# Four waits in the mixing stages and the order of the last down projection, in a two-layer hybrid backbone with expert-choice routing

## The chip, the cores and the metric

The kernel runs on one core of one Trainium2 chip. A time is device microseconds from the start to the end of one execution. The time before is the median of three runs; beside it there is one profiled execution, from which every row below comes.

## The reference

Two layers work on 512 latent tokens and 256 context tokens of width 1024, all in float32. Each layer mixes tokens and then routes them to 16 experts:

```python
for l in range(DEPTH):
    # six modulation vectors of each stream, from the conditioning
    mod = silu_c @ w_ada[l] + b_ada[l]
    mod_c = silu_cc @ w_ada[l] + b_ada[l]
    ...
    mix_c, st_f, st_b = token_mixer(xn_c @ w_in[l], ...)       # mLSTM, conv, Fourier
    h_ctx = h_ctx + cgt1 * (mix_c @ w_out[l])
    h_ctx = h_ctx + cgt2 * expert_choice_ffn(modulated_rmsnorm(h_ctx, ...), ...)
    mix_x, _, _ = token_mixer(xn @ w_in[l], ...)               # starts from st_f, st_b
    x = x + gt1 * (mix_x @ w_out[l])
    x = x + gt2 * expert_choice_ffn(modulated_rmsnorm(x, ...), ...)
return _rms(x, g_final)

def expert_choice_ffn(xn, w_router, w_gate, w_up, w_down):
    aff = softmax(xn @ w_router)
    gate, idx = top_k(aff.T, 2 * n // 16)      # 64 latent, 32 context tokens an expert
    hid = silu(xs @ w_gate) * (xs @ w_up)      # xs: the rows of xn at idx
    ys = (hid @ w_down) * gate
    return zeros_like(xn).at[idx].add(ys)
```

The last layer mixes the context only as far as its mLSTM states, and routes latent tokens alone.

## The kernel before

Each layer has four stages: the mixing with its input projection, the output projection with the residual, the routing (logits, softmax, the top tokens of each expert, the gather of their rows), and the experts in eight pairs.

**Who sets the order.** TensorE's instructions run in the order in which the code is written. The other engines' instructions are put in order by a scheduler that looks at dependencies and estimated costs, so a line can go much earlier or later than it stands. Each engine then runs its own list strictly in order: an instruction that waits holds up all behind it. Transfers are issued from SP's queue (weights in the main) and from POOL's queue (`w_ada`, the gate rows, gathers).

**Weights of the projections.** Each block of 128 columns of `w_in` or `w_out` is loaded by SP (L414), split into a high half on ScalarE (L422) and a low half on VectorE or, for some blocks, on POOL (L425), and multiplied by TensorE (L490). In layer 1 POOL makes the low half of every second block from number 4 to 15, in layer 0 from 12 to 19.

**The gates of the mLSTM.** A generator computes running sums and maxima of the gates with VectorE scans (L654, L656), then four exponentials on ScalarE (L680 to L690), and writes two results, M and WI, to a scratch tensor in DRAM from POOL's queue (L706, L707). They are fetched back later (L773). The key blocks are copied out of PSUM with a scale by ScalarE at L973.

**Fill work.** The modulation vectors are made from `w_ada` by small matmuls (L284, eight a yield in layer 0's out-projection; one result is copied at L290 and multiplied at L293). This work is a generator that runs between the blocks of other stages. An object of class `Fill` holds a credit: each block adds its time by a rate, and the generator runs while the credit is above zero. The vectors of layer 1 are made from layer 0's output projection on (`ada1`), and what is left of them runs in the routing.

**The output projection** goes over eight blocks `db`. Its residual line is L1177 on VectorE. L1108 scales the router's weights, which L1104 loads, for use on TensorE. Before the loop a tile Z of zeros is written on POOL (L1097) and sent to the accumulators `accl` and `accc` in DRAM (L1099, 3 MB in all); its place is then free for the next tile, which is that of the router's weights. The experts' outputs are added to these accumulators.

**The routing** ends with casts of the chosen indices on ScalarE (L1281, L1285), two small matmuls (L1288), index arithmetic on VectorE, gathers of the rows on POOL's queue (L1356), and TensorE's transposes of them (L1382).

**The experts.** Gate and up are L1433. A pair's two experts sit in the two halves of TensorE's columns (64 tokens each in layer 1), and gate and up take turns between them. `down_last` is the down projection of layer 1's last pair: four quarters `qd` of 256 output columns, 16 matmuls each (L1693). ScalarE scales a quarter out of PSUM (L1699), VectorE makes its low half (L1700). The sums into the residual are made by a permutation matmul for each block of 128 channels (L1498, two matmuls each) and L1499 on VectorE; `scat` is a list of such closures and `pop(scat, n)` runs n of them. ScalarE squares the result (L1675), and `rows` sums the squares on TensorE (L1683) for the final norm. L1693's loop over `k0` and `e` sets four matmuls of one expert, one popped closure, four of the other, another closure.

Of the kernel before, what the change touches and what calls it, by code (L numbers as in the profile page):

```python
# [50 lines left out]
NACC = 6  # L51
WORDER = [[KB0 + i for i in range(4)] + p + [QB + i for i in range(4)] + [FB, FB + 1] + [OB + i for i in range(4)]
# [103 lines left out]
def build(nc, tc, xT, ctxT, params, w_ada, w_gates, w_in, w_out, w_router, w_e_gate, w_e_up, w_e_down,  # L156
# [6 lines left out]
    def body(A, RB, PS, scr, xrow, acc):  # L163
# [233 lines left out]
        for l in range(2):  # L397
# [216 lines left out]
            keep = {}  # L614
            convq = []
# [18 lines left out]
            def chain():  # L634
# [45 lines left out]
                act.activation(DEC, DEC, AF.Exp)  # L680
# [4 lines left out]
                act.activation(WS, WS, AF.Exp)  # L685
                dve.tensor_tensor(FL, b_, M, OP.add)
                act.activation(FL, FL, AF.Exp, scale=-1.0)
                WI = b_
                dve.tensor_tensor(WI.rearrange("p (c t) -> p c t", c=6), MSb, M3, OP.subtract)
                act.activation(WI, WI, AF.Exp)  # L690
# [15 lines left out]
                pool.dma_start(scr[l, 0], M)  # L706
                pool.dma_start(scr[l, 1], WI)  # L707
# [258 lines left out]
            for h in range(H):  # L966
                ps = in_block(KB0 + h, seqs)
                for s in seqs:
                    o, v = tview(kT[:, h, OFF[s]:OFF[s] + LEN[s]], h, s), rview(ps[s], h, s)
                    if h < 2 and s == LAT:  # L970
                        dve.tensor_scalar(o, v, 128.0 ** -0.5, None, op0=OP.mult)
                    else:
                        act.activation(o, v, AF.Copy, scale=128.0 ** -0.5)  # L973
                done.add(f"k{h}")
                if h == 0 and l == 0:
                    areg = [mem.alloc(1024) for _ in range(4)]

                    def ada0():
                        for r in (1, 2):
                            yield from ada_round(0, r, Ring(areg), 5, pool, wloads[1:2] if r == 1 else (), some=ADS[0])  # L980
                        ada_scale(0, A2[0], 4, P_G2)

                    fills.append(Fill(ada0(), ADA0_RATE))
# [111 lines left out]
            if not last:  # L1095
                z_r, Z = new(512)
                pool.memset(Z, 0.0)  # L1097
                for s, a in ((LAT, 8), (CTX, 4)):
                    sp.dma_start(acc[s].rearrange("(p a) (b f) -> p (a b) f", p=128, f=512),  # L1099
                                 Z[:, None, :].to_broadcast([128, a, 512]))  # L1100
                mem.free(z_r)
# [11 lines left out]
            if not last:  # L1113
# [9 lines left out]
                ada1f = Fill(ada1(), ADA1_RATE)  # L1123
                fills.append(ada1f)


# [6 lines left out]
            wtiles, wtaken = [], [0]  # L1133

            def load_experts(firsts=(), most=1000):
                while len(wtiles) < min(wtaken[0] + len(wreg), len(wq), most):
                    w, e, i = wq[len(wtiles)]
                    if last and w is w_e_down and e >= E - 2:
# [3 lines left out]
                        for k0, k1 in ((0, KB),) if i < 3 else ((0, 4), (4, KB)):  # L1142
                            sp.dma_start(t[:, k0:k1], src[:, k0:k1])
# [17 lines left out]
            for db in range(KB):  # L1161
# [14 lines left out]
                for s in outs:  # L1176
                    dve.scalar_tensor_tensor(X[s][:, db], banks[s], MOD[l][:, s, 16 + db:17 + db], X[s][:, db],  # L1177
                                             op0=OP.mult, op1=OP.add)
                if db == 4:
                    ride(0)  # L1180
# [7 lines left out]
            mem.free([YT_r, wraw, wh, wl, wr_r, wra_r])  # L1188
# [473 lines left out]
            def down_last(p):  # L1662
# [23 lines left out]
                for qd in range(4):  # L1686
# [3 lines left out]
                    for k0 in (0, 4):  # L1690
                        for e in range(2):
                            for k in range(k0, k0 + 4):
                                pe.matmul(b[64 * e:64 * e + 64], hT[:, k, 64 * e:64 * e + 64], w[e][:, k],  # L1693
                                          start=k == 0, stop=k == KB - 1, tile_position=(0, 64 * e))
                            pop(scat)
                    pop(scat, 99)
                    c0 = qd * 256
                    h, lo = (YS[:, j, c0:c0 + 256] for j in range(2))
                    act.activation(h, b, AF.Copy, scale=GP[:, 0, p:p + 1])  # L1699
                    dve.scalar_tensor_tensor(lo, b, GP[:, 0, p:p + 1], h.bitcast(F32), op0=OP.mult, op1=OP.subtract)  # L1700
                    if qd == 2:
                        rows(range(4))
                    scat.extend(last_sum(db) for db in (2 * qd, 2 * qd + 1))
# [141 lines left out]
```

## Time and profile before

| | |
|---|---|
| median of three runs | 1856.98 us (1856.57 to 1857.13) |
| the profiled execution's own time | 1857.74 us |
| its span, first to last instruction | 1856.0 us |
| TensorE busy | 1744.3 us, 94% |
| VectorE, ScalarE, POOL busy | 627.9, 448.5, 166.0 us |
| mean granted clock of TensorE | 0.97 of 2.4 GHz |
| moved by DMA | 529.59 MB, mean 285 GB/s |

The span is 1.74 us shorter than the execution's own time: start and end around the instructions. The median is 0.76 us below the profiled execution. Layer 0's mixing lies at about 36 to 450 us, its routing to 482, its experts to 1035; layer 1's mixing runs to about 1340, and its experts to the end. Busy TensorE means that a matmul is in flight, not that the array is full.

### The profile page before, as it was taken

How to read it: one execution, taken by the hardware profiler on the slowest of the kernel's cores; microseconds unless marked ns; L12 is line 12 of the kernel's file. 1: busy time of each engine (PE TensorE's matmuls, PEld its weight loads, DVE VectorE, ACT ScalarE, POOL GpSimd, SP SyncE). 2: the span in 40 equal slices, each digit the busy share in tenths (PEclk: the TensorE clock that was granted, in tenths of full speed). 3: DMA queues.
4: the chain of work that ended last, by engine and by line, in shares of the span. 5: the costliest groups of instructions: out<-in, count | busy, mean ns of one | idle time of the engine just before them, and what ended most of it. 6: DMA issues, size and time to landing. Idle time of an engine off the chain costs nothing.

```text
span 1856.0 us, 27692 instructions
## 1 busy us (share of the span) xinstructions
PE 1744.3 (94%) x11728; PEld 947.8 (51%) x11728; DVE 627.9 (34%) x1384; ACT 448.5 (24%) x862; POOL 166.0 (9%) x193
## 2 busy tenths in 40 slices
PE   7899999899899999999999989889989999999997
PEld 3678887676333333333233468777644444334433
DVE  4624897323201001001014567956230221121213
ACT  5423354313201101101000553346221001110001
POOL 1122120321101101101100001110000000000000
PEclk8999999899899999999999999999989999999998
DMA  9365344855899999999995112233659999999992
GB/s 346 115 208 193 106 133 137 314 188 209 350 419 402 411 412 403 399 421 391 393 393 217 35 54 79 76 108 129 250 240 421 420 420 421 420 421 420 421 420 99
DMA packets 100668, 529.59 MB, mean 285 GB/s; under 512 B 10176, under 2 KB 21440, under 8 KB 51648
## 3 DMA queue, kind: packets, MB, share of 16 engines
q1 hardware_dynamic: 81920, 459.66, 61.8%
q0 software_dynamic: 18624, 68.17, 11.7%
q8 instruction: 92, 1.51, 0.3%
q14 instruction: 32, 0.26, 0.0%
HBM read 513.10 MB, written 14.68 MB: 284 GB/s over the span
## 4 chain that ended last, share of the span: by engine, by line
PE 70%; DMA 10%; DVE 9%; issue 5%; ACT 2%; SPq 2%; POOL 1%; another core or an unknown queue 0%; DVEq 0%; POOLq 0%; ACTq 0%
PE PS L1433 29%; PE PS L490 16%; PE PS L1443 8%; PE PS L1379 3%; DVE A L1015 2%; PE PS L1498 2%; PE PS L284 1%; PE PS L1693 1%; SPq L309 1%; DMA accc<-A 1%; DMA WP<-w_e_up 1%; DMA A<-w_e_up 1%; DMA A<-w_e_down 1%; DMA A<-w_e_gate 1%; DMA WP<-w_e_gate 1%
## 5 line engine op out<-in xcount | busy, mean ns | idle before, releaser
L490 PE MATMUL PS<-RA,RB 128*128 128x512 f32 (+1 forms) x2352 | 516.4, 367 | 23.6 <-ACT A L973 8.0
L1433 PE MATMUL PS<-A 128*32 128x512 f32 (+1 forms) x2256 | 428.1, 594 | 2.7 <-DMA A<-w_e_up 2.2
L490 PEld LDWEIGHTS PS<-RA,RB 128*128 128x128 f32 x2352 | 379.3, 194 | 99.3 <-issue 20.6
L1433 PE MATMUL PS<-WP,A 128*32 128x512 f32 (+1 forms) x2160 | 373.9, 597 | 0.7 <-DMA WP<-w_e_up 0.7
L1433 PEld LDWEIGHTS PS<-A 128*32 128x32 f32 (+1 forms) x2256 | 128.0, 121 | 224.9 <-issue 213.7
L1433 PEld LDWEIGHTS PS<-WP,A 128*32 128x32 f32 (+1 forms) x2160 | 107.0, 117 | 192.7 <-issue 187.6
L1443 PE MATMUL PS<-WP,A 128*32 128x512 f32 x816 | 112.5, 595 | 0.0
L1015 DVE SCALAR_TENSOR_TENSOR A<-A 128x783 f32<-128x783 f32 (+1 forms) x120 | 107.4, 921 | 0.1
L1499 DVE SCALAR_TENSOR_TENSOR A<-PS,A 128x512 f32<-128x512 f32 x80 | 57.5, 748 | 130.5 <-PE PS L1498 130.5
L1387 ACT ACTIVATE A<-PS,A 128x128 f32<-128x128 f32 x80 | 36.4, 457 | 262.0 <-DVE A L1389 260.8
L1486 ACT ACTIVATE A<-PS 128x512 f32<-128x512 f32 x40 | 23.8, 597 | 306.2 <-PE PS L1485 306.0
L1389 DVE TENSOR_SCALAR A<-PS,A 128x128 f32<-128x128 f32 x80 | 32.6, 409 | 185.8 <-PE PS L1382 93.4
L1443 PE MATMUL PS<-A 128*32 128x512 f32 x656 | 95.3, 607 | 0.0
L422 ACT ACTIVATE RB<-A 128x1024 fp32r<-128x1024 f32 x60 | 63.2, 1057 | 128.4 <-PE PS L490 83.1
L1532 DVE TENSOR_SCALAR A<-PS,A 128x512 f32<-128x512 f32 x6 | 4.5, 750 | 245.6 <-PE PS L1433 245.6
L282 POOL DMA_DIRECT2D A<-w_ada x80 | 60.1, 754 | 211.2 <-PE PS L284 134.2
L1506 DVE SCALAR_TENSOR_TENSOR RB<-PS,A,RB 128x512 fp32r<-128x512 f32 x18 | 13.5, 750 | 163.7 <-ACT RB L1505 162.8
L1379 PE MATMUL PS<-A 128*128 128x128 f32 x512 | 64.0, 285 | 5.0 <-DVE A L1499 4.5
L425 DVE TENSOR_TENSOR RB<-A,RB 128x1024 fp32r<-128x1024 f32 x50 | 60.8, 1221 | 21.0 <-ACT RB L422 20.6
L1379 PEld LDWEIGHTS PS<-A 128*128 128x128 f32 x512 | 61.0, 199 | 12.9 <-DVE A L1499 9.8
L1443 PEld LDWEIGHTS PS<-WP,A 128*32 128x32 f32 x816 | 26.8, 109 | 50.8 <-issue 50.8
L1498 PE MATMUL PS<-RB 128*128 128x512 f32 x160 | 51.7, 431 | 1.0 <-DVE A L1499 0.4
(334 smaller groups left out, 1583.8 us busy)
## 6 DMA issues: line engine op xcount, KB each, us to landing
A<-w_e_gate SPq DMA_DIRECT2D x75, 1024.0 KB, 14.3
A<-w_e_up SPq DMA_DIRECT2D x66, 1024.0 KB, 13.0
WP<-w_e_down SPq DMA_DIRECT2D x63, 1024.0 KB, 14.3
A<-w_e_down SPq DMA_DIRECT2D x63, 1024.0 KB, 16.0
WP<-w_e_up SPq DMA_DIRECT2D x62, 1024.0 KB, 13.0
WP<-w_e_gate SPq DMA_DIRECT2D x53, 1024.0 KB, 14.9
A<-w_ada POOLq DMA_DIRECT2D x80, 512.0 KB, 5.5
A<-w_in SPq DMA_DIRECT2D x44, 512.0 KB, 3.7
```

The costliest lines, as they stand in the source:

```text
L282: after(eng.dma_start(w, src[r, hf, k]), firsts if hf == 0 and k < len(ring.regs) else ())
L422: whi.append(act.activation(h, raw[i], AF.Copy))
L425: wlo.append(eng.tensor_tensor(lo, raw[i], h.bitcast(F32), OP.subtract))
L490: pe.matmul(banks[s][:, :LEN[s]], w[:, k], xin[:, j, k, OFF[s]:OFF[s] + LEN[s]], start=k == k0 and i == 0, stop=k == k1 and i == 2)
L1015: dve.scalar_tensor_tensor(o, i, wcol, o, op0=OP.mult, op1=OP.add)
L1379: pe.matmul(b[:, j], XT[2 + c][:, db * 128:db * 128 + 128], onehots[i][:, c], start=c == 0, stop=c == 3)
L1387: act.activation(dst[:, db], b[:, j], AF.Identity, bias=sh_, scale=sc_)
L1389: dve.tensor_scalar(dst[:, db], b[:, j], sc_, sh_, op0=OP.mult, op1=OP.add)
L1433: pe.matmul(B(o + hf)[c:c + wd, :], lhs(k, e)[:, c % 64:c % 64 + wd], w[e][:, a, hf * 512:hf * 512 + 512], start=k == 0, stop=k == KB - 1, ...
L1443: pe.matmul(B(o + 2)[32 * g:32 * g + 32, :], lhsc(k, e), w[e][:, a, hf * 512:hf * 512 + 512], start=k == 0, stop=k == KB - 1, tile_positio ...
L1498: pe.matmul(b, YS[:, j, db * 128:db * 128 + 128], PM if pm is None else pm, start=j == 0, stop=j == 1)
L1499: dve.scalar_tensor_tensor(X[LAT][:, db], b, MOD[l][:, LAT, 40 + db:41 + db], X[LAT][:, db], op0=OP.mult, op1=OP.add)
```

## The change

Five edits:

1. ScalarE's four exponentials of the gates are made to come after a key copy: the generator waits until `k1` is done, and each exponential has a dependency without a semaphore (an order for the scheduler) on the last key copy, which L973 records in `kev`.
2. The two transfers of M and WI are put behind the last splits that POOL has been given.
3. Z takes a place at the top of the memory that is not given to another tile until the end of the output projection. The two transfers of it are written in blocks 1 and 3 of that loop.
4. `ada1f` starts with a debt of 2.0 us of credit.
5. In `down_last` the two experts take turns at each `k`, and closures run after a quarter instead of within it. The loads of the last quarter's weights go half by half for both experts.

```diff
+ADA1_LATE = 2.0
...
+            kev = []
...
-                act.activation(DEC, DEC, AF.Exp)
+
+                while "k1" not in done:
+                    yield None
+                after(act.activation(DEC, DEC, AF.Exp), kev, NOSYNC)
...
-                act.activation(WS, WS, AF.Exp)
+                after(act.activation(WS, WS, AF.Exp), kev, NOSYNC)
...
-                pool.dma_start(scr[l, 0], M)
-                pool.dma_start(scr[l, 1], WI)
+                for j, t in enumerate((M, WI)):
+                    after(pool.dma_start(scr[l, j], t), [w for w in wlo[-2:] if w.ins.engine == mybir.EngineType.Pool], NOSYNC)
...
-                        act.activation(o, v, AF.Copy, scale=128.0 ** -0.5)
+                        kev[:] = [act.activation(o, v, AF.Copy, scale=128.0 ** -0.5)]
...
-            if not last:
-                z_r, Z = new(512)
-                pool.memset(Z, 0.0)
-                for s, a in ((LAT, 8), (CTX, 4)):
-                    sp.dma_start(acc[s].rearrange("(p a) (b f) -> p (a b) f", p=128, f=512),
-                                 Z[:, None, :].to_broadcast([128, a, 512]))
-                mem.free(z_r)
...
+                ada1f.credit = -ADA1_LATE
                 fills.append(ada1f)
 
+            if not last:
+                z_r, Z = new(512, top=True)
+                pool.memset(Z, 0.0)
...
-                        for k0, k1 in ((0, KB),) if i < 3 else ((0, 4), (4, KB)):
-                            sp.dma_start(t[:, k0:k1], src[:, k0:k1])
+
+                        halves.append((t, src))
+                        if i < 3:
+                            sp.dma_start(*halves.pop())
+                        elif len(halves) == 2:
+                            for k0 in (0, 4):
+                                for t_, s_ in halves:
+                                    sp.dma_start(t_[:, k0:k0 + 4], s_[:, k0:k0 + 4])
...
+                if db in (1, 3) and not last:
+
+                    s, a = ((LAT, 8), (CTX, 4))[db // 2]
+                    sp.dma_start(acc[s].rearrange("(p a) (b f) -> p (a b) f", p=128, f=512),
+                                 Z[:, None, :].to_broadcast([128, a, 512]))
...
-                    for k0 in (0, 4):
+
+                    for k in range(KB):
                         for e in range(2):
-                            for k in range(k0, k0 + 4):
-                                pe.matmul(b[64 * e:64 * e + 64], hT[:, k, 64 * e:64 * e + 64], w[e][:, k],
-                                          start=k == 0, stop=k == KB - 1, tile_position=(0, 64 * e))
-                            pop(scat)
-                    pop(scat, 99)
+                            pe.matmul(b[64 * e:64 * e + 64], hT[:, k, 64 * e:64 * e + 64], w[e][:, k],
+                                      start=k == 0, stop=k == KB - 1, tile_position=(0, 64 * e))
...
+                    if qd == 0:
+                        pop(scat, 99)
...
-                    if qd == 2:
+                    if qd == 3:
                         rows(range(4))
+                    pop(scat, 99)
```

In the changed kernel the lines have other numbers: L284 is L285 there, L290 is L291, L293 is L294, L1099 is L1191, L1104 is L1102, L1281 is L1295, L1285 is L1299, L1288 is L1302, L1382 is L1396, L1498 is L1512, L1683 is L1697 and L1693 is L1707.

TensorE's list from the last logits transposes to the gather's transposes in layer 0's routing, first before and then after the change:

```order
L1242 MATMUL PS_70<-A_63,WP4_3275 96x128 x2
L1266 MATMUL PS_70<-A_63 128x128 x48
L284 MATMUL PS_70<-A_63 32x256 x16
L1288 MATMUL PS_70<-A_63,WP5_3276 128x96 x2
L284 MATMUL PS_70<-A_63 32x256 x40
L293 MATMUL PS_70<-A_63 128x8 x4
L1382 MATMUL PS_70<-A_63,WP5_3276 128x128 x8
```

```order
L1256 MATMUL PS_70<-A_63,WP4_3258 96x128 x2
L1280 MATMUL PS_70<-A_63 128x128 x48
L294 MATMUL PS_70<-A_63 128x8 x4
L285 MATMUL PS_70<-A_63 32x256 x8
L1302 MATMUL PS_70<-A_63,WP5_3259 128x96 x2
L285 MATMUL PS_70<-A_63 32x256 x56
L294 MATMUL PS_70<-A_63 128x8 x4
L1396 MATMUL PS_70<-A_63,WP5_3259 128x128 x8
```

One group of L294 has moved from the output projection to the place ahead of L1302, with eight L285 behind it, and 56 instead of 40 stand between L1302 and the transposes. On ScalarE the copy L291 for that first group stands between the two L1295.

TensorE's list in the last down projection, from its first quarter into its second, before and after (WP0 to WP2 and A are the places of the weights):

```order
L1485 MATMUL PS_70<-A_63 128x128 x8
L1693 MATMUL PS_70<-A_63 64x256 x4
L1498 MATMUL PS_70<-RB_64 128x512 x2
L1693 MATMUL PS_70<-WP0_8537,A_63 64x256 x4
L1498 MATMUL PS_70<-RB_64 128x512 x2
L1693 MATMUL PS_70<-A_63 64x256 x4
L1693 MATMUL PS_70<-WP0_8537,A_63 64x256 x4
L1693 MATMUL PS_70<-WP1_8538,A_63 64x256 x4
```

```order
L1707 MATMUL PS_70<-A_63 64x256
L1707 MATMUL PS_70<-WP0_8537,A_63 64x256
L1512 MATMUL PS_70<-RB_64 128x512 x4
L1707 MATMUL PS_70<-WP1_8538,A_63 64x256
L1707 MATMUL PS_70<-WP2_8539,A_63 64x256
L1707 MATMUL PS_70<-WP1_8538,A_63 64x256
L1707 MATMUL PS_70<-WP2_8539,A_63 64x256
```

After the change the first two rows are repeated eight times ahead of the four sums, and so are the pairs of the later quarters; no sum stands within a quarter any more.

SP's list from the start, before and after:

```order
L309 DMA A_63<-w_ada 128x4x256 x8
L414 DMA A_63<-w_in 128x1024 x2
L309 DMA A_63<-w_ada 128x4x256 x8
L414 DMA A_63<-w_in 128x1024 x14
L883 DMA A_63<-dft_ch 128x256
```

```order
L310 DMA A_63<-w_ada 128x4x256 x8
L415 DMA A_63<-w_in 128x1024 x2
L310 DMA A_63<-w_ada 128x4x256 x8
L415 DMA A_63<-w_in 128x1024 x2
L1191 DMA accl_68<-A_63 1024x1x512
L1191 DMA accc_69<-A_63 512x1x512
L415 DMA A_63<-w_in 128x1024 x12
L888 DMA A_63<-dft_ch 128x256
```

The two transfers of zeros now stand behind the fourth load of w_in instead of just ahead of the router's weights. On POOL's list in layer 1 both transfers to `scr` now stand behind two splits, where before the first of them stood ahead of the first split and the second ahead of the second.

## Rows read from the trace of the kernel before

**Rows 1.** The page's part 2: tenths of TensorE's busy time, and GB/s.

```profile
PE   7899999899899999999999989889989999999997
...
GB/s 346 115 208 193 106 133 137 314 188 209 350 419 402 411 412 403 399 421 391 393 393 217 35 54 79 76 108 129 250 240 421 420 420 421 420 421 420 421 420 99
```

**Rows 2.** The chain that ended last, around the last pair: start, us, what.

```profile
1792.34 3.82 PE PS L1433 x16
...
by line: PE PS L1693 45.4%; PE PS L1498 11.9%; DVE A L1747 8.4%; PE PS L1683 4.8%; PE PS L376 3.7%; DVE A L1499 2.7%; PE PS L1433 2.3%; PE PS L359 1.9%; DVE RB L1700 1.8%; ACT RB L1699 1.7%; DVE A L375 1.6%; issue 1.6%; PE PS L1485 1.2%; DV
...
1804.02 1.94 PE PS L1693 x8
1805.96 0.66 PE PS L1498 x2
...
1809.16 2.80 PE PS L1693 x16
...
1812.56 0.49 DVE RB L1700
...
1836.95 0.98 PE PS L1683 x4
...
1838.63 0.76 DVE A L1499
...
1840.15 1.72 PE PS L1683 x4
```

**Rows 3.** L1693's own instructions: weight loads, ns min/median/max.

```profile
L1693 PEld LDWEIGHTS PS<-WP,A x96: 132/137/137, 1806.6 to 1835.4; 128*64 128x64 f32 x96
```

**Rows 4.** The chain that ended last, 325 to 365 us.

```profile
329.04 21.76 DMA accc<-A
...
350.88 7.25 DMA A<-w_router
```

**Rows 5.** Waits, 325 to 365 us: us in total, times, longest.

```profile
PE PS L490 <- DVE A L1177: 4.4, 1, 4.4
...
PE PS L284 <- DMA A<-w_ada: 3.8, 2, 2.9
```

**Rows 6.** Transfers, 0 to 70 us, in 40 slices of 1.75 us.

```profile
GB/s 0 186 305 375 391 362 391 384 387 384 386 384 393 420 393 385 384 389 373 382 404 413 379 370 349 201 5 0 0 0 0 0 0 5 0 227 169 213 187 360
```

**Rows 7.** Timeline of the routing: start, us, instructions, idle before and its releaser.

```profile
466.10 0.63 ACT L1281 ACTIVATE WP<-WP 32x128 f32<-32x128 f32 x2 [1.47 <-DVE WP L1249]
...
467.10 0.39 PE L1288 MATMUL PS<-A,WP 96*128 96x96 f32 x2 [1.63 <-ACT WP L1285]
...
467.41 4.52 PE L284 MATMUL PS<-A 128*32 128x256 f32 x80
...
470.18 1.06 POOL L1356 DMA_INDIRECT WP<-xrow,A  x1 [19.93 <-DVE A L1322]
...
474.63 0.60 ACT L290 ACTIVATE A<-PS 128x512 f32<-128x512 f32 x1 [7.59 <-remote]
...
475.28 1.45 PE L293 MATMUL PS<-A 128*128 128x8 f32 x8 [3.34 <-ACT A L290]
...
476.58 1.95 PE L1382 MATMUL PS<-A,WP 128*128 128x128 f32 x8
```

**Rows 8.** Timeline of the second split in layer 1's mixing.

```profile
1099.65 1.08 ACT L422 ACTIVATE RB<-A 128x1024 fp32r<-128x1024 f32 x1
...
1107.57 2.70 POOL L425 TENSOR_TENSOR RB<-A,RB 128x1024 fp32r<-128x1024 f32 x1
1107.99 2.30 DVE L679 TENSOR_TENSOR A<-A 128x6 f32<-128x6 f32 x1
...
1110.32 7.05 PE L490 MATMUL PS<-RA,RB 128*128 128x512 f32 x22 [5.03 <-POOL RB L425]
...
1114.15 1.23 DVE L425 TENSOR_TENSOR RB<-A,RB 128x1024 fp32r<-128x1024 f32 x1 [2.12 <-ACT RB L422]
```

**Rows 9.** TensorE's waits, 84 to 102 us.

```profile
PE PS L490 <- ACT A L973: 6.8, 1, 6.8
```

More of the change, by code (lines that the diff above doesn't have):

```diff
@@ L684, in chain @@
                                   ML[:, :, None].to_broadcast([128, 6, 128]), OP.subtract)
-                act.activation(WS, WS, AF.Exp)
+                after(act.activation(WS, WS, AF.Exp), kev, NOSYNC)
                 dve.tensor_tensor(FL, b_, M, OP.add)
-                act.activation(FL, FL, AF.Exp, scale=-1.0)
+                after(act.activation(FL, FL, AF.Exp, scale=-1.0), kev, NOSYNC)
                 WI = b_
                 dve.tensor_tensor(WI.rearrange("p (c t) -> p c t", c=6), MSb, M3, OP.subtract)
-                act.activation(WI, WI, AF.Exp)
+                after(act.activation(WI, WI, AF.Exp), kev, NOSYNC)
                 while KGO[l] not in done:
@@ L1132, in body @@
             wq = [(w, 2 * q + e, i) for w, q in order for i in range(4) for e in range(2)]
-            wtiles, wtaken = [], [0]
+            wtiles, wtaken, halves = [], [0], []
             def load_experts(firsts=(), most=1000):
@@ L1187, in body @@
             fills.clear()
-            mem.free([YT_r, wraw, wh, wl, wr_r, wra_r])
+            mem.free([YT_r, wraw, wh, wl, wr_r, wra_r] + ([] if last else [z_r]))
             ra_close()
```

## The prediction

> **What bounds the kernel now.** I read the page's forty slices first [rows 1]. TensorE is at 9 tenths or more in all but nine (46.4 us each): 1, 2 and 8 in layer 0's mixing, 11 with the routing, 24, 26 and 27 in layer 1's mixing, 30 with its routing, and the tail. From slice 31 the transfers stand flat at 420 GB/s, so layer 1's experts are bound by their weights, while in layer 0's experts TensorE never waits. Both stages run as long wherever they begin: time taken out of the mixing before them moves all that follows, and time taken out of the last down projection, after the stream has ended, comes off the end directly. So I price four places, each by the wait that ends last there: layer 0's out-projection, the routing behind it, the splits in layer 1, and the last down. The profiled execution took 1857.74 us, 0.76 above the median of 1856.98; I make the sum on the profile and take 0.76 off.
>
> **The last down, the largest term.** The chain over the last pair [rows 2] shows four quarters of 16 matmuls (64x256; each leaves two records, so x8 is four matmuls). Four matmuls of one expert standing alone, x8, take 1.94, 0.47 each. Eight, four of one expert and then four of the other, take 2.80: the second four add only 0.9. The two experts sit in different column halves, and the halves overlap where both have work queued. Before, the order offers that only partly: a block of one expert, two full-width sums of 0.66, a block of the other, two more sums, then both blocks. L1693 makes 45.4% of these 56 us, 25.4, or 6.35 a quarter, and a quarter's four sums 1.33. The nearest row for full alternation is in the same view: eight 64x512 matmuls of gate or up, alternating, x16, take 3.82. That is as many columns as 16 of 64x256, so I price a quarter at 3.75 and the downs at 15.0 against 25.4, 10.4 less.
>
> Not all of that stays, because the sums lose their cover. My walk from 1804.02, which is unchanged: quarter 0 to 1807.8; four sums (1.33) to 1809.1; quarter 1 shares quarter 0's bank and must wait until VectorE's L1700 has read it. Before, this wait was 1.1 (1811.96 to the 0.49 at 1812.56 and its end); now two updates of 0.76 (L1499) stand in front of that read, so I let it begin at 1810.4. Quarter 1 to 1814.1; sums to 1815.4; quarter 2 to 1819.1; sums to 1820.4; the same wait to 1820.9; quarter 3 to 1824.6. Then four row sums L1683 (0.98), four sums (1.33) to 1826.9, a round trip of L1499, a square (L1675) and row sums that used to lie under matmuls, about 2.4 to 1829.3, the last sums to 1830.6, and the final L1683, after its update, at 1831.5. Before, that one began at 1840.15. **Term: -8.6**, bounds -6.5 (each round trip 1 us longer) and -10.4 (none shows). The last slice, from 1809.6, moves 99 GB/s over 46.4 us, 4.6 MB, of which 2.1 are the result; the other 2.5 are weights, 6 us at 420 GB/s [rows 1]. So the weights are in by 1816, ahead of quarter 3 at 1820.9; if the reordered last halves came after that, each us late would cost one.
>
> Here a rule counts against the change. Each matmul loads its own weights, 64 columns in 132 ns [rows 3]. In the alternating rows 16 loads would add 2.1 to 3.82 if they were exposed, and the row has no room for them, so I count them as hidden. The Trainium skill (TensorE: Matmul & The Clock Gate, part 3, What overlaps and what doesn't) says that a weight load overlaps matmuls in flight only when the row group differs, and these pairs use all rows. By it the gain would be about nil here; the 3.82 of this trace disagrees with it. This is the second rival below.
>
> **Zeros in an own place.** Before, the zeros for the accumulators go out near 329, behind a memset that waits for TensorE; the second transfer lands 21.76 after issue, and the router's weights, whose tile takes the place of the zeros, go only at 350.88 and land 7.25 later [rows 4]. VectorE scales them, L1177 stands behind on its queue, and TensorE waits 4.4 for it [rows 5]. After, the router's load has no such wait and is issued at about 329: on nobody's path. **Term: -4.4**, bounds 0 (something else holds L1177 as long) and -4.4. The zeros, 3 MB, now stand on SP's queue behind four early loads of w_in and ahead of all others. The DMA engines carry next to nothing from about 46 to 60 us, since the tiles of the next w_in are not free yet [rows 6]. So the 3 MB, at the 21.76 they took beside other traffic, fit before the next w_in load at about 60. Cost 0; without that cover, up to 21.8 (the third rival).
>
> **Vectors' fill later.** TensorE waits 3.8 for w_ada in two places [rows 5]: the fill's first loads were issued just before, and the zeros are moving at the same time [rows 4]. The debt of 2.0 at a rate of 0.3 puts the first yield some 7 us later, and the zeros are gone from there. **Term: -3.8**, bounds -2 and -3.8. One group of the fill, 8 of L284 (113 ns each [rows 7]) and four of L293 (at most 1.45 there, I take 1.0), leaves the out-projection, where TensorE is busy: **-1.9**, bounds -1 and -2.3.
>
> They come back in the routing. Before, TensorE's L1288, which passes the chosen indices on, started at 467.10 as soon as ScalarE's casts were done. After, four L294 and eight L285 stand ahead of it on TensorE, and the L294 wait for a copy (0.60) that ScalarE does between the two casts: 466.10 + 0.31 + 0.60, 467.0. So L1302, the same line, starts at 467.0 + 1.2 for L294 + 0.9, near 469.1, 2.0 late, and with it the gather (before: issued from 470.18, used at 476.58 [rows 7]). **Term: +2.1**, lower bound +1.5. The 56 L285 behind it end at 469.6 + 56 x 0.113 = 475.9, the copy and the last L294 near 478.0, inside the gather's new end of 478.7. But before, the copy at 474.63 came 2.7 after the last L284 (467.41 + 4.52) for a reason the trace does not name; if that hold comes again the drain ends at 480.7 and the term is +4.1, the upper bound.
>
> **Rows out behind the splits, in layer 1.** POOL had its queue blocked by L706, which waits for VectorE; behind it stood the split L425, whose input was ready at 1100.7. It ran at 1107.57 for 2.70, and TensorE waited 5.03 for it [rows 8]. After, the splits stand first, so this split can end at 1103.4 and TensorE goes on at 1105.3. But what is late next is the following block's low half, VectorE's L425 at 1114.15 to 1115.4, behind the exponentials; TensorE finishes the earlier block by about 1110.3 and stops there instead. It resumes earlier only if VectorE's chain does. While POOL's split ran, VectorE's L679, of six columns, took 2.30 and ended with it. Move the split to 1100.7 and an operation there is held instead: the scans of the gates. Then VectorE ends as late as before and the gain is 0; if the scans are not held, 2.2. The row with the held operation is nearer, so **-0.4**, bounds 0 and -2.2. The Trainium skill (SBUF — State Buffer, the section on the ports) has the shared port pair as an exclusive lock for a GpSimd operation that reads SBUF and a VectorE operation with two inputs there; scans are of that kind, so by it the term is 0. The 2.30 agrees with it. In layer 0 the rows out keep their place among the same instructions; the first fetch of them moves behind fourteen w_ada issues, still ahead of the second fetch: 0.
>
> **Exponentials behind key copies.** The order shows ScalarE's exponentials between the same key copies in both layers as before. In layer 0 TensorE's 6.8 for the copy L973 [rows 9] is what it was meant for, and the copy still stands behind them: **0**, bounds 0 and -1.
>
> **Sum**: -8.6 - 4.4 - 3.8 - 1.9 + 2.1 - 0.4 = -17.0. On the profile 1840.7, as a median **1840.0**. All best ends together give about -23, all worst ones -5.
>
> **Rivals.** (1) *The freed time returns in the routing and in layer 1.* The held copy makes the routing +4.1, the fill gives back only 2 of its 3.8 and VectorE holds TensorE in layer 1 as long as before: -17.0 + 2.0 + 1.8 + 0.4 = -12.8, 1844.2; with the router's 4.4 gone as well 1848.6. For it: the unexplained 2.7, and that three of these places wait on one another. Against: the router's wait has a clear releaser. (2) *The last down's loads are exposed.* 64 loads of 0.132 cost 8.4 and the sums no longer fill gaps: -0.2 in place of -8.6, 1848.4. For: the rule above, and the L1693 blocks are not the L1433 ones. Against: the x16 in 3.82, and the 0.9 that a second expert's four add. (3) *Slower: the zeros hold up layer 0's first weights.* If they do not leave before w_in is free but wait with lanes still held by w_ada, all of 21.8 stands in front of the load at 60 us: 1840.0 + 21.8 = 1861.8. It decides from the point where they land later than about 60; each us beyond costs one, and from 17 beyond on the change loses. Against: some 13 us of idle DMA there. (4) *The change does not do what it says*, as with the exponentials, for both large terms: about 1853 to 1857.
>
> **How the numbers follow.** Forecast (within some 4 us of 1840): 0.62. Rival 1: 0.17. Rival 2: 0.10. Both of these together or 4, near 1853: 0.07. Rival 3: 0.04. From rivals 1 and 2 the range reaches to 1849; below, the better bounds to 1834. A measurement of this kernel can tell 0.2%, 3.7 us. Faster than 1853.3: 0.62 + 0.17 + 0.10 + 0.04 = 0.93; within: 0.03; slower: 0.04.
>
> **What would show it.** Right: the chain of the last pair with x32 in about 3.7 and the final L1697 some 8.6 after less time; no wait of TensorE for the scaled router weights or for w_ada near 340; the gather's first issue 2 us further from the last MAX8; TensorE's wait for POOL in layer 1 replaced by one for VectorE or ScalarE. Wrong: a quarter of the last down above 5 us, weight loads on its path, waits for w_in before 65 us, or a routing that is more than 4 us longer.

## The result, and the profile after

The changed kernel takes 1841.68 us (median of 4 runs, 1834.89 to 1843.91) against 1857.06 before (4 runs): a ratio of 0.9898, with a 95% interval of 0.9863 to 0.9932. The forecast was 1840.0. That the sum is this close is luck, since errors in it cancel: the out-projection gave 5 us more than priced, and the start of layer 0, priced at nothing, and the routing took 7.6 more. The prediction also took 0.2% as what a measurement can tell; over the batches below single times of the kernel before went from 1847.46 to 1862.06, so edits are compared here by stages, and medians only where they lie well apart.

The profiled execution, the slowest of the four, took 1843.91 us, its span 1842.1, 13.9 less than before. The table sets the same TensorE instructions of each trace side by side; a stage is the time from the start of one such matmul to that of the next, so its number comes from two rows. Stages that the edits leave alone scatter too: layer 0's experts took 543 to 546 us in all executions, whatever the edits.

| stage (us in the trace before) | before | after | down_only | zeros_ old_place | fill_at_ once | ada_loads_ after | all_ mended |
|---|---|---|---|---|---|---|---|
| to the first blocks (0 to 45.5) | 45.5 | 51.2 | 44.9 | 50.0 | 51.0 | 43.7 | 43.8 |
| rest of the mixing (45.5 to 336) | 290.6 | 289.7 | 289.5 | 289.8 | 289.7 | 289.3 | 289.9 |
| out-projection, first blocks (336 to 375) | 38.9 | 23.4 | 39.4 | 37.3 | 25.6 | 23.1 | 25.5 |
| its other blocks (375 to 448) | 72.6 | 73.2 | 71.7 | 73.0 | 71.8 | 70.6 | 71.8 |
| routing up to L1288 | 19.6 | 23.5 | 19.6 | 23.5 | 19.5 | 22.6 | 19.5 |
| on to the experts | 15.5 | 15.7 | 13.3 | 14.6 | 13.3 | 14.5 | 15.6 |
| layer 1: split and block after it (1098 to 1147) | 49.7 | 49.6 | 49.8 | 49.6 | 49.9 | 49.6 | 49.8 |
| last down up to the last row sums | 42.0 | 33.2 | 33.2 | 33.2 | 33.2 | 33.2 | 33.2 |

The page's part 2 after the change, TensorE's busy tenths and GB/s, answers to [rows 1]; from slice 31 on the stream of weights stands at 420 to 422 as it did, up to the last slice:

```profile
PE   5989999998999999999999998889979999999996
...
GB/s 361 159 192 204 93 123 182 226 201 252 344 419 402 410 414 403 395 421 396 391 401 222 35 46 86 69 118 97 240 238 421 421 420 420 420 422 420 420 421 175
```

**The last down.** The chain that ended last, at the end of the changed kernel (start, us, what; L1707 is the former L1693 and L1697 the former L1683), answers to [rows 2]:

```profile
1787.31 3.85 PE PS L1447 x16
...
1799.01 3.67 PE PS L1707 x32
...
1804.87 0.40 DVE RB L1715
...
1805.32 3.67 PE PS L1707 x32
...
1810.12 3.60 PE PS L1707 x32
...
1815.63 3.67 PE PS L1707 x32
1819.31 0.99 PE PS L1697 x8
...
1826.34 1.72 PE PS L1697 x4
```

A quarter's 16 matmuls, x32, take 3.67 instead of 6.35 on average. L1707's weight loads after the change (ns min/median/max) are as long as in [rows 3]:

```profile
L1707 PEld LDWEIGHTS PS<-WP,A x96: 132/137/137, 1799.0 to 1818.7; 128*64 128x64 f32 x96
...
L1707 PEld LDWEIGHTS PS<-A x32: 133/137/137, 1799.0 to 1818.7; 128*64 128x64 f32 x32
```

That is 32 loads a quarter, two for each matmul as there are two records of it. One behind the other they would take 4.2 to 4.4, more than the whole quarter does, so most of them run beside other work. The last L1697 starts 27.3 after the first L1707, where before it was 36.1.

**The out-projection.** Its timeline on TensorE after the change:

```profile
340.41 7.80 PE L491 MATMUL PS<-RA,RB 128*128 128x512 f32 x42
348.13 1.07 PE L285 MATMUL PS<-A 128*32 128x256 f32 x16
349.13 3.74 PE L491 MATMUL PS<-RA,RB 128*128 128x256 f32 x21
```

There is no gap: both waits of [rows 5] are gone, and L491 runs from 340.41 on. Two windows of before show what the waits had cost besides (after the window and its length come the busy us, with the instructions, of TensorE, its weight loads, VectorE, ScalarE and POOL, then TensorE's granted clock, the DMA share and GB/s):

```profile
335.00:345.00 10.00, 6.14 (x32) 3.50 (x31) 5.63 (x11) 3.33 (x8) 4.48 (x6) 0.71 1.03 401
...
355.00:365.00 10.00, 5.61 (x34) 3.62 (x33) 3.04 (x5) 1.88 (x3) 1.01 (x2) 0.83 0.73 257
```

The same columns after:

```profile
335.00:345.00 10.00, 9.91 (x66) 8.73 (x65) 9.79 (x22) 8.22 (x16) 5.47 (x8) 1.00 0.97 317
345.00:355.00 10.00, 10.00 (x77) 7.31 (x77) 3.67 (x5) 2.00 (x3) 2.72 (x4) 1.00 0.98 331
```

With the waits the granted clock was 0.71 and 0.83 of 2.4 GHz over these windows, and behind them, from 339.3 to 346.0 and from 360.0 to 364.0, 0.50 and 0.61; now it is full. What that cost can be read from fill_at_once below, which runs the same 204 records of TensorE in the first blocks without either wait: 25.6 against 38.9. Of the 13.3 between them 8.2 are the waits, and the other 5.2 are matmuls that ran slowly, most of them behind the waits.

**The routing.** The timeline of the changed kernel, answering to [rows 7]:

```profile
456.33 0.57 ACT L291 ACTIVATE A<-PS 128x512 f32<-128x512 f32 x1
...
456.95 1.87 PE L294 MATMUL PS<-A 128*128 128x8 f32 x8 [3.33 <-ACT A L291]
...
459.24 1.94 PE L285 MATMUL PS<-A 128*32 128x256 f32 x16 [0.42 <-DVE A L296]
...
461.11 0.58 PE L1302 MATMUL PS<-A,WP 96*128 96x96 f32 x2
...
464.38 1.06 POOL L1370 DMA_INDIRECT WP<-xrow,A  x1 [24.07 <-DVE A L1336]
...
469.88 0.60 ACT L291 ACTIVATE A<-PS 128x512 f32<-128x512 f32 x1 [12.32 <-PE PS L285]
```

The window around L294, with the granted clock behind the engines:

```profile
455.00:462.00 7.00, 4.63 (x30) 2.87 (x34) 2.54 (x11) 1.40 (x4) 0.00 (x0) 0.55 0.36 139
```

As priced, L294 waits for the copy L291 between the two casts. But after the 3.33 us in which TensorE waited, its granted clock is 0.55 in this window: L294 takes 1.87 and the 16 records of L285 take 1.94, where full clock gives 1.07. L1302 comes 3.9 later than before, counted from the end of the out-projection, and POOL's first gather with it.

**Layer 1's splits**, with the rows that answer to [rows 8]:

```profile
1094.45 2.60 POOL L426 TENSOR_TENSOR RB<-A,RB 128x1024 fp32r<-128x1024 f32 x1 [22.11 <-ACT RB L423]
1094.86 2.47 DVE L656 TENSOR_TENSOR_SCAN A<-A 64x128 f32<-64x128 f32 x1
1097.34 0.42 DVE L658 TENSOR_TENSOR_SCAN A<-A 64x128 f32<-64x128 f32 x1
...
1109.64 1.65 PE L491 MATMUL PS<-RA,RB 128*128 128x512 f32 x3 [5.66 <-ACT A L1000]
```

The split runs as soon as its input is there, the scan that it meets takes 2.47 in place of 0.42, and TensorE's wait has moved to L1000, a read of PSUM that stands behind the exponentials on ScalarE.

**The start.** No wait of TensorE before 60 us was in the sum. This is POOL's first load of the next w_ada in the timeline of before:

```profile
32.45 1.68 POOL L282 DMA_DIRECT2D A<-w_ada  x2 [30.43 <-DMA A<-w_ada]
```

And TensorE's last matmuls for the first modulation vectors, also before:

```profile
41.19 0.64 PE L311 MATMUL PS<-A 128*32 128x256 f32 x8 [1.17 <-DMA A<-w_ada]
```

POOL's timeline after the change:

```profile
29.04 3.17 POOL L283 DMA_DIRECT2D A<-w_ada  x4 [26.55 <-DMA A<-w_ada]
```

TensorE's timeline after:

```profile
39.65 1.08 PE L312 MATMUL PS<-A 128*32 128x256 f32 x8 [5.15 <-DMA A<-w_ada]
...
46.91 0.64 PE L312 MATMUL PS<-A 128*32 128x256 f32 x8
```

And its waits up to 450 us after (total, times, longest):

```profile
PE PS L312 <- DMA A<-w_ada: 7.4, 3, 5.1
...
PE PS L491 <- ACT A L978: 6.8, 1, 6.8
```

TensorE now waits 7.4 for the weights of the first modulation vectors (L312, formerly L311), whose last matmuls start at 46.9 instead of 41.2. The wait of [rows 9] is what it was.

### The profile page after: what moved, and what is told of

Its sections match the earlier page's. It is cut to its first block, busy times and chain, and to the rows that moved or that the text cites. A ratio compares the mean times of both kernels' runs of the same rounds, so it can differ in the third digit from the quotient of the medians.

```text
span 1842.1 us, 27682 instructions
## 1 busy us (share of the span) xinstructions
PE 1728.1 (94%) x11728; PEld 937.4 (51%) x11728; DVE 627.6 (34%) x1384; ACT 448.8 (24%) x862; POOL 164.5 (9%) x193
## 5 line engine op out<-in xcount | busy, mean ns | idle before, releaser
L491 PE MATMUL PS<-RA,RB 128*128 128x512 f32 (+1 forms) x2352 | 512.3, 365 | 19.7 <-ACT A L978 8.0
L491 PEld LDWEIGHTS PS<-RA,RB 128*128 128x128 f32 x2352 | 375.9, 192 | 93.9 <-issue 20.8
L1500 ACT ACTIVATE A<-PS 128x512 f32<-128x512 f32 x40 | 23.8, 597 | 305.9 <-PE PS L1499 305.8
L1512 PE MATMUL PS<-RB 128*128 128x512 f32 x160 | 50.5, 428 | 1.0 <-DVE A L1513 0.4
## 6 DMA issues: line engine op xcount, KB each, us to landing
A<-w_e_gate SPq DMA_DIRECT2D x75, 1024.0 KB, 13.9
WP<-w_e_gate SPq DMA_DIRECT2D x53, 1024.0 KB, 13.9
```

What stands on the lines that cost most here:

```text
L491: pe.matmul(banks[s][:, :LEN[s]], w[:, k], xin[:, j, k, OFF[s]:OFF[s] + LEN[s]], start=k == k0 and i == 0, stop=k == k1 and i == 2)
L1512: pe.matmul(b, YS[:, j, db * 128:db * 128 + 128], PM if pm is None else pm, start=j == 0, stop=j == 1)
```

## The experiments

My first theory of the start was the third rival's: the zeros, now at 38 us, hold up the loads beside them. Its own rival was that another edit moves other loads.

**down_only.** The kernel before with the fifth edit alone, the diff's parts on `halves` and in `down_last`:

```diff
-                    for k0 in (0, 4):
+                    for k in range(KB):
                         for e in range(2):
-                            for k in range(k0, k0 + 4):
-                                pe.matmul(b[64 * e:64 * e + 64], ...)
-                            pop(scat)
+                            pe.matmul(b[64 * e:64 * e + 64], ...)
```

> The kernel before with the last edit alone: the two experts take turns in the last down projection, sums run after a quarter, and the last weights come half by half. If the last down is worth what the trace after shows, the time from the first of its matmuls to the last row sums is 9 to 10 us shorter and the kernel is near 1847.5. If part of it is owed to the other edits, it gains 5 or less, 1852 or more. Nothing ahead of the last pair may differ from before.

Measured: 1842.92 us, ratio 0.9937 (0.9902 to 0.9972). The last down is 8.8 shorter, as with all edits. The median is lower than 1847.5 by stages that the edit does not touch: in the profiled execution layer 0's experts took 2.4 less, and a hold of 2.3 behind the routing was missing. That part of the median is scatter.

**zeros_after_ada.**

```diff
+        adone = []
...
+                adone.append(act.activation(rows, ps[:, hf * 256:hf * 256 + 256], AF.Copy))
...
-                    sp.dma_start(acc[s]..., Z...)
+                    after(sp.dma_start(acc[s]..., Z...), adone[-1:])
```

> The changed kernel, with the two transfers of zeros waiting for the last copy of the first modulation vectors, so that they move in the gap in which the DMA engines are idle. If it is the zeros that hold back the first w_ada loads in the changed kernel, TensorE's wait there falls from 7.4 to about 1.3 and the kernel gains 5.5 to 7.5: about 1835. If that wait has another cause (the order of the w_ada issues on POOL, chance), it stays and the time is that of the changed kernel, about 1841.

Measured: 1838.16, ratio 0.9898 (0.9868 to 0.9927). The zeros go at 48.5, after all of it, and the last L312 still starts at 47.2: the part up to 45 us is as long as in the changed kernel. My theory of the zeros falls.

**zeros_old_place.** The third edit undone, the others kept:

```diff
+            if not last:
+                z_r, Z = new(512)
+                pool.memset(Z, 0.0)
+                for s, a in ((LAT, 8), (CTX, 4)):
+                    sp.dma_start(acc[s]..., Z...)
+                mem.free(z_r)
             cs0 = OFF[outs[0]] // 128
...
-                if db in (1, 3) and not last:
-                    ...
```

> The changed kernel with the zeros as before: Z in the place of the router's weights, its transfers just ahead of them. If both readings of the zeros are right, the start loses its 6 us of delay and the out-projection gets back the 4.4 for the router's weights and some 2 us more at a lower clock: 1841 to 1843, so that the edit on the zeros by itself is worth nothing. If the early zeros cost nothing, it is 1846 to 1848.

Measured: 1847.06, ratio 0.9944 (0.9926 to 0.9962). The start is late here too, without early zeros. In the out-projection the wait for the router's weights comes back, and larger, since the waits for w_ada no longer lie ahead of it:

```profile
PE PS L491 <- DVE A L1190: 11.9, 1, 11.9
```

Its first blocks take 37.3 against 23.4: the edit on the zeros is worth 13.9 there.

**fill_at_once.**

```diff
-ADA1_LATE = 2.0
+ADA1_LATE = 0.0
```

> The changed kernel without the debt of the vectors' fill. The routing has its former order again, with no copy between the casts, and should take 4 us less. If the two waits for w_ada at the fill's first matmuls came from the zeros beside them, they are gone by now and the kernel is near 1837.5. If they come from the fill's start in itself, 3.8 us and some 2 us of lower clock return and the time is 1842 to 1843.5.

Measured: 1835.07, ratio 0.9873 (0.9842 to 0.9904). No wait for w_ada is left in the out-projection without the debt either, and of the edits that are left only the one on the zeros bears on this place: the zeros beside the loads had caused it. The debt shortens the first blocks of the out-projection by 2.1, by work that it moves, and lengthens the routing up to the indices by 4.0 and what follows by 2.4. The first two hold in all traces (the first blocks take 23.0 to 23.8 with the debt and 25.5 to 26.1 without, where no long wait stands in them; the routing 22.5 to 23.5 and 19.5 to 19.6); what follows scatters from 13.0 to 15.7 with or without it.

**no_key_order.** What differs at the start between all these and down_only is when POOL's first loads go. In the list of POOL, the loads of the next w_ada wait for matmuls 43 to 55 of TensorE's list with the first edit, and for 49 to 63 without it. ScalarE's order there is the same. By the two programs, the generator that waits for `k1` takes its tiles later, so that the four tiles of those loads come to lie over others, which are free sooner.

```diff
-                while "k1" not in done:
-                    yield None
-                after(act.activation(DEC, DEC, AF.Exp), kev, NOSYNC)
+                act.activation(DEC, DEC, AF.Exp)
```

(and the other three alike)

> The changed kernel without the edit on the exponentials (neither the wait for k1 nor the order behind the key copies). In the program this changes no order on ScalarE, but the four tiles into which POOL loads the next w_ada come to lie where they did before, so that these loads wait for matmuls 49 to 63 and not 43 to 55. If the 6 us that the changed kernel loses by 45 us come from these loads starting 3.5 us early, the first part up to 45 us falls from 32.3 to 25 to 27 and the kernel gains about 6: 1834 to 1836. If they come from the early zeros or from another edit, the part stays above 30.

Measured: 1836.50, ratio 0.9906 (0.9870 to 0.9942). The expectations from here on count the part up to 45 us from 19 us on: 26.3 before, 32.3 after. It is 30.1 here, between the two, and so inconclusive. POOL's loads start at 30.83 here, since TensorE itself was faster in this execution; its last L312 starts at 44.6. Two things make up the 3.4 by which the loads start earlier in the changed kernel than before. In each trace the first goes 0.3 after the end of the matmul that it waits for: matmul 49 before, which ends at 32.1, and matmul 43 in the changed kernel, which ends at 28.7. (The profile names a load of w_ada as what ended that wait, but TensorE had already used its tile.) In the changed kernel matmul 49 ends at 29.8, so what the edit did is worth 1.1 there; the other 2.3 are a lead of TensorE itself, and where that comes from stays open.

**ada_loads_held** and **best_of_these.** One line more, and in the second also the two mends above:

```diff
-    yield from ada_round(0, r, Ring(areg), 5, pool, wloads[1:2] if r == 1 else (), some=ADS[0])
+    yield from ada_round(0, r, Ring(areg), 5, pool, wloads[1:2] + adone[:1] if r == 1 else (), some=ADS[0])
```

> The changed kernel with all its edits; only POOL's first load of w_ada also waits for the copy of the first half of the first modulation vectors (at about 33). This takes the early start away and leaves the placement and the order behind the key copies. If the start of these loads is the cause, the part up to 45 us falls to 25 to 28 and the kernel to about 1835. If it is the placement by itself, the part stays at 30 to 32.

> The changed kernel with three mends: POOL's loads held as in ada_loads_held, zeros after the first modulation vectors, no debt of the fill. Each stage by itself: start 25 to 27, out-projection 25.5, the routing up to the chosen indices 19.5 in place of 23.5. If the stages add up, 6 us for the start and 2 for fill and routing come off the changed kernel's 1841.7: 1831 to 1834. If they trade against each other, 1835 or more.

Measured: 1833.83, ratio 0.9875 (0.9833 to 0.9916), and 1832.74, ratio 0.9888 (0.9852 to 0.9925). The first tells nothing on the cause. The hold did act: the loads start 0.3 after the copy has ended, some 2 later than after matmul 43. But with TensorE further ahead the copy itself ends at 29.3, so the loads start at 29.6, hardly later than in the changed kernel, and the part up to 45 us takes 33.0. In the second they start at 31.2, with the last L312 at 43.7 and the part at 29.1.

**ada_loads_after** and **all_mended.** `adone[1:2]` in place of `adone[:1]`, that is, behind the second half; all_mended has the late zeros and no debt as well.

> The changed kernel, with POOL's first four loads of w_ada held until the copy of the second half of the first modulation vectors, so that none of them stands among the loads that TensorE waits for. In ada_loads_held the copy it waited for was done by 29.5 and held nothing. Over the runs so far the last of these matmuls starts the later, the earlier POOL's loads begin (41.2 for 32.5, 43.7 for 31.2, 45.7 for 30.0, 47.2 for 28.4). If that is the cause, it now starts by 41 at the latest, or by 39 since nothing of POOL's is ahead, the part up to 45 us is 23 to 27, and the kernel comes to 1833 to 1836. If the early zeros are what holds the loads back, it stays beyond 44.

> The changed kernel with POOL's loads held as in ada_loads_after, zeros behind the first modulation vectors and no debt of the fill. By stages: 23 to 26 up to 45 us, 25.5 for the out-projection, 19.5 for the routing up to the chosen indices: 8 to 10 less than the changed kernel, 1830 to 1833. If 5 MB in the gap before 60 us are too much, w_in is late and the part from 45 to 100 us is longer than 54.

Measured: 1826.76 us (1825.20 to 1828.32), ratio 0.9835 (0.9806 to 0.9863), and 1833.02 us (1829.27 to 1836.60), ratio 0.9865 (0.9841 to 0.9889). POOL's timeline in ada_loads_after:

```profile
40.83 3.23 POOL L283 DMA_DIRECT2D A<-w_ada  x4 [5.62 <-ACT A L319]
```

TensorE's:

```profile
39.43 0.64 PE L314 MATMUL PS<-A 128*32 128x256 f32 x8
```

SP's, with the zeros:

```profile
33.29 0.61 SPq L1194 DMA_DIRECT2D accl<-A  x1
```

And TensorE's waits for w_ada up to 60 us:

```profile
PE PS L314 <- DMA A<-w_ada: 1.1, 2, 0.7
```

POOL's loads wait until 40.83, the last matmul starts at 39.43, and TensorE waits 1.1 in place of 7.4, although the zeros go out as early as 33.29. The part up to 45 us takes 24.4, and 25.0 in all_mended. So it was POOL's loads, and not the zeros. Nor is it that TensorE was ahead: in all_mended matmul 47 starts at 28.75, in the changed kernel at 28.92, and the start is short all the same. Nothing from 45 to 100 us is longer in either kernel, so 5 MB do fit into the gap. ada_loads_after beats the kernel before and the changed one. That all_mended, which mends more, came out slower is on record (each of its six times lies above all four of the other) and only in part explained: its profiled execution is 6.6 longer, 2.9 of it in layer 0's experts, which neither edit touches, and 1.6 from the out-projection to the experts, where 3.1 less in the routing do not make up for the work that comes back and for the hold described below. So dropping the debt on top of held loads is not shown to gain.

**down_blocks.** The changed kernel with the former order of matmuls, and still no sum within a quarter:

```diff
-                    for k in range(KB):
+                    for k0 in (0, 4):
                         for e in range(2):
-                            pe.matmul(b[64 * e:64 * e + 64], ...)
+                            for k in range(k0, k0 + 4):
+                                pe.matmul(b[64 * e:64 * e + 64], ...)
```

> The changed kernel with the former order within a quarter of the last down (four matmuls of one expert, four of the other), and the sums after the quarter as changed. Read is the time of a quarter's 16 matmuls. If a block's matmuls wait in line for their column half and the other half works meanwhile, a quarter is the changed 3.67 plus one block's lead of 0.9, 4.6: most of the last down's gain is owed to the sums that no longer stand within. If only turns at each k overlap, a quarter takes 6.5 or more.

**down_turns_with_sums.** Turns, but with sums inside a quarter again. The output of this kernel is not the reference's, for a reason that stays open; it has the same number of TensorE instructions and is read for its time alone:

```diff
                             pe.matmul(b[64 * e:64 * e + 64], hT[:, k, 64 * e:64 * e + 64], w[e][:, k],
                                       start=k == 0, stop=k == KB - 1, tile_position=(0, 64 * e))
+                        if k in (1, 3):
+                            pop(scat)
```

> The changed kernel with the experts taking turns at each k, but with a sum after the second and the fourth k of a quarter. In down_blocks a quarter without sums inside takes 4.6 in place of 3.67. If each interruption empties the column halves and costs one matmul's lead, 0.25 to 0.5, a quarter's 16 matmuls take 4.2 to 4.7 beside the sums. If only the order of the experts counts, 3.7.

Measured: 1843.78 and 1837.43 us. The chain that ended last, of down_blocks:

```profile
1795.13 4.70 PE PS L1708 x32
```

And of down_turns_with_sums:

```profile
1792.82 1.08 PE PS L1707 x8
1793.91 0.67 PE PS L1512 x2
1794.58 1.01 PE PS L1707 x8
1795.59 0.67 PE PS L1512 x2
1796.26 1.90 PE PS L1707 x16
```

In blocks a quarter takes 4.70, and the stage 37.3: taking the sums out of the quarter is worth 4.7 of the 8.8. With turns and sums inside, a quarter's pieces of L1707 add to 3.99, and the stage is 33.3, as short as with the sums outside. The turns alone give it all: the two sums between the pieces cost these 0.3 together, and what they cost up to the last quarter (it starts 18.0 after the first L1707, against 16.6 in the changed kernel) comes back behind it (9.4 against 10.7 to the last L1697), where fewer sums are left.

**rows_out_first.** The second edit undone:

```diff
-                for j, t in enumerate((M, WI)):
-                    after(pool.dma_start(scr[l, j], t), [w for w in wlo[-2:] if w.ins.engine == mybir.EngineType.Pool], NOSYNC)
+                pool.dma_start(scr[l, 0], M)
+                pool.dma_start(scr[l, 1], WI)
```

> The changed kernel without the edit on POOL's rows out. In layer 1 TensorE should wait some 5 us for POOL's split again, and the other wait, for ScalarE behind the exponentials, should be gone. If one only takes the place of the other, the time from the block before the split to 1147 us is within 0.7 of the changed kernel's (49.6); if the edit is worth its wait, it is 2 to 5 longer.

Measured: 1838.59. Its wait in layer 1:

```profile
PE PS L491 <- POOL RB L426: 5.0, 1, 5.0
```

The wait for POOL is back, the one for L1000 is gone, and the stage takes 49.8 against 49.6. One wait takes the place of the other.

## Why the prediction was right, and where it was not

- **Last down, -8.6.** Measured -8.8, in every kernel with the turns. The price of a quarter (3.75 against 3.67) and the walk over the waits held. The second rival had the loads exposed; the x32 in 3.67 leaves no room for 32 loads of 132 to 137 ns. The rival counted 64 loads, one a matmul; the trace has 128, so its price would have been 17 and not 8.4. The rule of the Trainium skill (TensorE: Matmul & The Clock Gate, part 3, What overlaps and what doesn't) has a load overlap matmuls only where the row group differs; this trace disagrees with it.
- **Zeros, -4.4, and fill, -3.8 and -1.9: mis-sized.** The three terms together came to -15.4 instead of -10.1. Nearly all of the difference, 5.2, is the granted clock: I took the waits out at their own length (8.2) and the matmuls behind them at the speed they had, but most of these had run slowly, at 0.50 to 0.61, because TensorE had waited. And the terms were put down to the wrong edits. The zeros explain both waits (without the debt 13.3, by fill_at_once; 13.9 with it, by zeros_old_place); the debt gives 2.1 of moved work (fill_at_once).
- **Routing, +2.1: mis-sized.** +3.9 up to L1302, from the same oversight: L294 and L285, priced at 1.2 and 0.9, took 1.87 and 1.94 at half clock, with an unpriced wait of 0.42 between them. The upper bound of +4.1 stood on another cause, the hold of 2.7 before the copy. That hold shows in the traces of before and all_mended and not in down_only, fill_at_once and best_of_these, which have the same order there; where it is missing (fill_at_once) the debt costs 6.4 in the routing. Its cause stays open.
- **Rows out behind the splits, -0.4.** Right in size (-0.1, and -0.2 by rows_out_first) and in the mechanism but for one name. The scan that POOL's split meets took 2.47 in place of 0.42, and TensorE waits 5.66 behind the exponentials in place of 5.03 for POOL. What ends this wait is ScalarE's L1000 and not VectorE's low half, which I had named and which starts at 1107.71 and is done 0.7 earlier. The Trainium skill (SBUF — State Buffer, Who interferes with whom) says that a VectorE instruction with two inputs in SBUF contends with a POOL instruction that reads there; the 2.47 agrees.
- **Exponentials, 0: the step that failed.** I read that ScalarE's order does not change, which is so, and concluded that nothing does. The wait for `k1` also changes when tiles are taken, hence where four others lie and which matmuls POOL's loads wait for. They go 3.4 us earlier, beside loads that TensorE needs first, and the start is 5.7 longer. That POOL's loads cause it is shown by holding them; how much of it is this edit's is not, since 2.3 of the 3.4 are TensorE's own lead, and undoing the edit alone took 2.2 of 6.0 off the part. I had read each queue's order but only ScalarE's waits for this edit; POOL's stood in the same list.
- **The slower rival** named the right place, the first loads of layer 0, but the wrong transfer. Zeros at 33 to 38 us cost nothing that shows at the start.

Over the span: +5.7 at the start, -0.8 in the rest of the mixing, -15.4 and +0.6 in the out-projection, +3.9 and +0.1 in the routing, -0.5 in layer 0's experts, +1.3 in layer 1, -8.8 in the last down: -13.9.

## What to carry to other kernels

Where two weight sets sit in two column halves of TensorE, let their matmuls take turns one by one: it took a quarter here from 6.35 us to 3.99 with other matmuls between the pieces, and from 4.70 to 3.67 without. When a wait goes or comes, price the matmuls behind it anew and not at the speed they had: behind waits of 3.3 and 4.4 us the granted clock was 0.50 to 0.61 here, and behind those of 1.1 and 1.5 in the last down it was full. And an edit that only delays when code takes a tile can move other tiles: compare what each transfer waits for, before and after, on the queues that the edit does not name, since an early load can be worse than a late one.

## What was not expected of the hardware

- Transfers on one queue delayed loads of another that were issued shortly before them or beside them. Over the executions the last L312 starts the later, the earlier POOL's four loads begin: 39.4 for 40.8, 40.3 for 32.9, 41.2 for 32.5, 43.7 for 31.2, 44.6 for 30.8, 45.7 for 30.0; for seven starts between 27.0 and 29.6 it is 46.1 to 47.6, with no order among them. The last of SP's loads for it begins at 28.7 to 30.1. SP's loads land 7.7 to 9.5 after their issue in down_only, where POOL's begin at 32.85, and 7.8 to 14.1 in zeros_old_place, where they begin at 29.95. The Trainium skill (DMA: Bandwidth & Descriptors, Queues, rings and completion order) has each DMA engine go round between the queues that have work; that POOL's 2 MB take a share from SP's agrees with it, and so does that the zeros, on SP's own queue behind those loads, do not.
- After 3.3 us of waiting, TensorE's granted clock was 0.55 over seven us, and the same 16 matmul records took 1.94 instead of 1.07.
